# A hybrid decoder layer on one core: gate tiles moved ahead of and behind a block inverse, gate sends moved to ScalarE, HGRN's early decays moved last in order, and down weights loaded into four idle slots

## The chip, the core and the metric

The kernel runs on one core of one Trainium2 chip. The core has TensorE for matrix products, VectorE and ScalarE for elementwise work, GpSimd, and queues from which transfers are started: SyncE's, ScalarE's and GpSimd's. All operands are float32; a product of two of them is made of three matmuls on "hi" and "lo" parts (rounded value and remainder) in a reduced float32 format. The metric is device time of one execution in microseconds (us); lower is better.

## What is computed

One decoder layer on 512 tokens of width 1024. Two causal mixers run on the same normalised input, a gated linear recurrence (HGRN2) and a gated delta rule (DeltaNet), both in 4 heads of 128. Their outputs are projected, weighted with the sigmoid gates `m_a` and `m_b`, added, projected again and put on the residual; a gated feed-forward part of width 2816 follows.

```python
u = rms_norm(x, pre_mix_w)
(hg_q, hg_f, hg_i, hg_g, dn_q, dn_k, dn_v, dn_g, dn_a, dn_b, m_a, m_b) = split(u @ w_in)
o_a = head_rms_norm(hgrn2_mix(hg_q, hg_f, hg_i, lb), hg_norm_w) * silu(hg_g)
cq, ck, cv = split(silu(causal_short_conv([dn_q, dn_k, dn_v], conv_w)))
o_b = head_rms_norm(gated_deltanet_mix(cq, ck, cv, dn_a, dn_b), dn_norm_w) * silu(dn_g)
merged = sigmoid(m_a) * (o_a @ w_o_hg) + sigmoid(m_b) * (o_b @ w_o_dn)
h = x + rms_norm(merged @ w_out, post_mix_w)
gate, up = split(rms_norm(h, pre_ffn_w) @ w_gate_up)
out = h + rms_norm((silu(gate) * up) @ w_down, post_ffn_w)
```

DeltaNet needs, for each chunk of the sequence and each head, the inverse of a unit triangular matrix.

## The kernel before

**Dense tiles.** `dense_in(name, evac, fts=...)` makes tiles of 128 output columns by 512 tokens. Each takes 24 matmuls of 512 columns (8 blocks of the inner dimension, three each: lines 124 and 125), a weight block of 512 KB that `wload` brings into one of two `raw` buffers by SyncE's queue and splits into `whi` (a cast on ScalarE, line 116) and `wlo` (a subtraction on VectorE, line 117), and an evacuation `evac`. `self.log[name]` keeps the matmuls. `dn_k`, `hg_f`, `dn_q`, `dn_v`, `dn_g`, `hg_q`, `hg_g`, `m_b0`, `m_b1`, `m_a0`, `m_a1` are such groups of four tiles; `y_proj` makes `y0` (DeltaNet's output projection) and `y1` (HGRN's) of eight tiles with 12 matmuls each.

**Order.** A scheduler of the framework sets each engine's instruction order at build time from the program order, `high_priority` and `issue_after` (this instruction comes behind that one in the order; not a wait on the chip). On the chip each engine runs its own list in order and waits on semaphores. Small matmuls of the mixers stand between dense ones. The inverse (`dn_inv`) puts each of its 28 groups of products (line 493, and transposes, line 520) behind every third matmul of the list it is given. HGRN's matmuls are put behind every fifth dense matmul of the list `dense` (`FIRST`, `PACE`, `paced`).

**Around the inverse.** `dn_sub` inverts blocks of 32 on GpSimd, a long chain of small operations on one tile; the result goes to DRAM (lines 474, 476) and comes back into the two tiles that `dn_inv` multiplies (lines 497, 500), all on GpSimd's queue. `dn_prep(c)` makes the scaled operands of DeltaNet for chunk c (lines 548, 552); `dn_step(c)` is the serial recurrence (lines 568 to 588, with ScalarE copies at 573 and 578 and the state update on VectorE at line 157); `head_norm` ends it with a column sum on TensorE (lines 389, 390), and `y0` needs its output of all chunks. `hg_prep` makes HGRN's cumulative decays (lines 624 to 641), `hg_decay` one level of its decay factors (line 654). `hg_attn` and `hg_step` are HGRN's matmuls (lines 690 to 732).

**Sends.** Gate and query tiles that come before their place is free go through one spill tile `out` to DRAM (`early_q`, `early_g`, `early_b`, `early_a`) and are read back later by GpSimd's queue. `early_q` is sent by ScalarE's queue (line 795), the others by GpSimd's (lines 801, 828).

**Down projection.** `down` takes 22 weight rows of 512 KB twice, once per half of the tokens; the last four of the second pass are split into `held` tiles. Each row is loaded into one of the two `raw` buffers; a row's 12 matmuls are lines 1204 to 1206, the left operand is cast at line 1194.

The lines that set the inverse's place, the early HGRN work and the paced list are:

```python
last = self.dn_inv((self.log["hg_q"] + self.log["hg_g"])[60::3])
with self.tc.issue_after(last.ins), self.tc.issue_after(norm[1].ins):
    self.hg_prep((2, 3))
    early_e = {lev: self.hg_decay(0, lev) for lev in HG_LEVELS[:5]}
...
dense = self.log["hg_g"][48:] + self.log["y0"] + self.log["m_b1"] + self.log["m_a0"]
self.marks = iter(dense[FIRST::PACE])
```

Of the kernel before, what the change touches and what calls it, by code (L numbers as in the profile page):

```python
# [25 lines left out]
NEG = -30000.0  # L26
FIRST, PACE = 8, 5
# [20 lines left out]
class K:  # L48
# [58 lines left out]
    def wload(self, src, shape, offs=(0, 0)):  # L107

        nc = self.nc
        n = shape[1] * shape[2]  # L110
        with self.tc.high_priority():
            raw = self.wp.tile([P, 1024], F32, tag="raw", name=self.name("raw"), bufs=2)
            hi, lo = (self.wp.tile([P, WCOLS], F32R, tag=t, name=self.name(t), bufs=3)[:, o:o + 1024]
                      for t, o in zip(("whi", "wlo"), offs))
            nc.sync.dma_start(out=raw[:, :n], in_=src)
            nc.scalar.copy(hi[:, :n], raw[:, :n])  # L116
            nc.vector.tensor_tensor(out=lo[:, :n], in0=raw[:, :n], in1=hi[:, :n].bitcast(F32),  # L117
                                    op=ALU.subtract)
        r = lambda t: t[:, :n].rearrange("p (a b) -> p a b", a=shape[1])
        return r(hi), r(lo)  # L120
# [632 lines left out]
    def mixers(self):  # L753
# [23 lines left out]
        with self.tc.issue_after(norm[0].ins), self.tc.issue_after(norm[1].ins):  # L777
# [12 lines left out]
                                              for n, t in ((4, "q"), (2, "g"), (4, "b"), (4, "a")))  # L790
# [6 lines left out]
        def gge(i, ps):  # L797
            t = self.spill()
            self.sigmoid(t, ps)
            self.stt(t, ps, self.hnw, t, ALU.mult, ALU.mult)  # L800
            nc.gpsimd.dma_start(out=early_g[i], in_=t)
# [6 lines left out]
        last = self.dn_inv((self.log["hg_q"] + self.log["hg_g"])[60::3])  # L808
        with self.tc.issue_after(last.ins), self.tc.issue_after(norm[1].ins):
            self.hg_prep((2, 3))  # L810
            early_e = {lev: self.hg_decay(0, lev) for lev in HG_LEVELS[:5]}
# [10 lines left out]
        run(prev)  # L822

        def gate_out(to):
            def f(ft, ps):
                t = self.spill()
                self.sigmoid(t, ps)
                nc.gpsimd.dma_start(out=to[ft], in_=t)
            return f

        self.dense_in("m_b0", gate_out(early_b))
# [25 lines left out]
        self.dense_in("m_a0", gate_out(early_a))  # L857
        dense = self.log["hg_g"][48:] + self.log["y0"] + self.log["m_b1"] + self.log["m_a0"]
# [14 lines left out]
        nc.gpsimd.dma_start(out=self.ma[0], in_=early_a.rearrange("f p t -> p f t"))  # L873
        self.dense_in("m_a1", lambda ft, ps: self.sigmoid(self.ma[1][:, ft, :], ps))
# [36 lines left out]
    def out_proj(self):  # L911
# [47 lines left out]
        for c in range(NC_):  # L959
# [9 lines left out]
            cut = ((0, 6), (1, 6), (0, 8), (1, 8)) if c == 0 else ((0, 8), (1, 4), (2, 0), (1, 8))  # L969
# [211 lines left out]
    def down(self):  # L1181
# [25 lines left out]

        def load(k):

            with self.tc.issue_after(made[k - 2].ins) if k > 1 else nullcontext():  # L1210
                return [x[:, 0] for x in self.wload(self.I["w_down"][k], (P, 1, D))]
# [37 lines left out]
        for k in range(NF):  # L1249
            a = left(k, 1)  # L1250
            if k < NF - KT:
                w = load(k)
            else:
                i = k - NF + KT
                with now():
                    raw = self.wp.tile([P, 1024], F32, tag="raw", name=self.name("raw"), bufs=2)
                    nc.sync.dma_start(out=raw, in_=self.I["w_down"][k])
                    w = [held[j][i // 2][:, i % 2] for j in range(2)]
                    self.split(*w, raw)
                late.append((a, w))  # L1260
# [35 lines left out]
    def run(self):  # L1296
        for f in (self.consts, self.start, self.mixers, self.merge, self.out_proj, self.ffn, self.down):
            f()
# [56 lines left out]
```

## Time and profile before

| what | us |
|---|---|
| time, median of 3 runs (lowest, highest) | 843.47 (842.88, 844.0) |
| the profiled execution, its own time | 843.4 |
| its span, first to last instruction | 841.6 |
| TensorE busy in the span (96%) | 811.4 |
| VectorE busy (69%) | 581.6 |
| ScalarE busy (58%) | 490.0 |
| GpSimd busy (10%) | 86.7 |

The span starts with the loads and the normalisation, the mixers run to about 412 us, the output projection and the feed-forward part follow, and the down projection runs from 700 us to the end. A matmul's busy time as recorded overlaps that of the next, so a TensorE that looks busy may still lose time; the distance between the starts of two matmuls tells more.

### The profile page before, as it was taken

How to read it: one execution, taken by the hardware profiler on the slowest of the kernel's cores; microseconds unless marked ns; L12 is line 12 of the kernel's file. 1: busy time of each engine (PE TensorE's matmuls, PEld its weight loads, DVE VectorE, ACT ScalarE, POOL GpSimd, SP SyncE). 2: the span in 40 equal slices, each digit the busy share in tenths (PEclk: the TensorE clock that was granted, in tenths of full speed). 3: DMA queues.
4: the chain of work that ended last, by engine and by line, in shares of the span. 5: the costliest groups of instructions: out<-in, count | busy, mean ns of one | idle time of the engine just before them, and what ended most of it. 6: DMA issues, size and time to landing. Idle time of an engine off the chain costs nothing.

```text
span 841.6 us, 12290 instructions
## 1 busy us (share of the span) xinstructions
PE 811.4 (96%) x4677; PEld 682.7 (81%) x4677; DVE 581.6 (69%) x943; ACT 490.0 (58%) x917; POOL 86.7 (10%) x126
## 2 busy tenths in 40 slices
PE   9999999799998899999999999999999999999995
PEld 8878888666877678888888898999999998877764
DVE  4794998313955798964574697887887787557545
ACT  5748789436857456767644464655555457445443
POOL 1000068600002000005010300000000000000000
PEclk9999999979999899999999999999999999999998
DMA  8425442622224111257511313233423405556552
GB/s 305 173 76 199 122 130 79 156 92 69 95 93 150 51 51 51 76 182 244 176 62 50 123 45 122 85 104 114 125 76 100 151 22 171 173 176 209 176 176 100
DMA packets 36699, 103.77 MB, mean 123 GB/s; under 512 B 4448, under 2 KB 4864, under 8 KB 36512
## 3 DMA queue, kind: packets, MB, share of 16 engines
q1 hardware_dynamic: 32112, 88.65, 32.0%
q0 software_dynamic: 3952, 13.29, 5.5%
q10 hardware_dynamic: 576, 1.05, 0.4%
q8 instruction: 37, 0.61, 0.3%
q14 instruction: 22, 0.18, 0.1%
HBM read 94.57 MB, written 8.40 MB: 122 GB/s over the span
## 4 chain that ended last, share of the span: by engine, by line
PE 63%; DMA 14%; DVE 10%; ACT 5%; POOL 5%; issue 3%; DVEq 0%; SPq 0%; ACTq 0%; POOLq 0%
PE mm L124 18%; PE mm L125 9%; DMA raw<-in_w_down_dram 8%; POOL s L154 4%; DVE wlo L117 3%; PE hps L124 3%; DVE s L154 3%; ACT whi L116 2%; PE hps L1090 2%; PE hps L1089 2%; PE hps L1091 2%; DVE s L157 2%; PE hps L697 2%; PE mm L947 2%; PE mm L945 2%
## 5 line engine op out<-in xcount | busy, mean ns | idle before, releaser
L124 PE MATMUL mm<-s,whi 128*128 128x512 f32 (+1 forms) x992 | 317.5, 394 | 6.2 <-ACT s L128 5.8
L124 PEld LDWEIGHTS mm<-s,whi 128*128 128x128 f32 x992 | 184.2, 190 | 43.1 <-ACT s L128 6.6
L117 DVE TENSOR_TENSOR wlo<-raw,whi 128x1024 fp32r<-128x1024 f32 x108 | 133.2, 1233 | 124.3 <-ACT whi L116 123.0
L125 PE MATMUL mm<-s,wlo 128*128 128x512 f32 (+1 forms) x496 | 193.4, 390 | 0.0
L116 ACT CAST whi<-raw 128x1024 fp32r<-128x1024 f32 x108 | 113.3, 1049 | 78.1 <-DMA raw<-in_w_down_dram 34.8
L125 PEld LDWEIGHTS mm<-s,wlo 128*128 128x128 f32 x496 | 94.6, 191 | 16.6 <-DVE wlo L117 0.4
L128 ACT CAST whi<-s 128x512 fp32r<-128x512 f32 x42 | 26.0, 618 | 45.5 <-PE mm L124 21.0
L128 ACT CAST whi<-raw 128x512 fp32r<-128x512 f32 x56 | 34.0, 618 | 25.9 <-PE mm L1090 9.5
L1090 PE MATMUL hps<-s,whi 128*128 128x256 f32 x168 | 46.5, 277 | 0.6 <-DVE s L154 0.6
L1089 PE MATMUL hps<-s,whi 128*128 128x256 f32 x168 | 46.5, 277 | 0.4 <-DVE hct L154 0.4
L1091 PE MATMUL hps<-s,wlo 128*128 128x256 f32 x168 | 46.4, 276 | 0.0
L124 PE MATMUL hps<-s,whi 128*128 128x512 f32 (+1 forms) x144 | 40.3, 366 | 0.0
L154 DVE TENSOR_TENSOR wlo<-raw,whi 128x512 fp32r<-128x512 f32 x56 | 37.9, 687 | 1.7 <-ACT whi L128 1.0
L154 DVE TENSOR_TENSOR s<-s,s 128x512 fp32r<-128x512 f32 (+2 forms) x51 | 35.7, 711 | 2.9 <-ACT s L128 1.7
L154 POOL TENSOR_TENSOR s<-s,dct 128x256 f32<-128x256 f32 x1 | 1.2, 1208 | 353.1 <-DVE s L157 353.1
L154 POOL TENSOR_TENSOR s<-s 128x126 f32<-128x126 f32 (+22 forms) x62 | 35.1, 566 | 9.7 <-DMA s<-scr 4.9
L128 ACT CAST s<-s 128x512 fp32r<-128x512 f32 (+1 forms) x32 | 19.8, 620 | 24.6 <-DVE s L154 17.6
L1090 PEld LDWEIGHTS hps<-s,whi 128*128 128x128 f32 x168 | 31.5, 188 | 1.1 <-DVE s L154 0.8
L1089 PEld LDWEIGHTS hps<-s,whi 128*128 128x128 f32 x168 | 31.5, 188 | 0.8 <-DVE hct L154 0.6
L1091 PEld LDWEIGHTS hps<-s,wlo 128*128 128x128 f32 x168 | 31.5, 188 | 0.0
L1089 PE MATMUL mm<-s,whi 128*128 128x256 f32 x112 | 31.0, 276 | 0.0
L1091 PE MATMUL mm<-s,wlo 128*128 128x256 f32 x112 | 31.0, 276 | 0.0
(316 smaller groups left out, 1819.6 us busy)
## 6 DMA issues: line engine op xcount, KB each, us to landing
raw<-in_w_in_a_dram SPq DMA_DIRECT2D x44, 512.0 KB, 3.5
raw<-in_w_down_dram SPq DMA_DIRECT2D x44, 512.0 KB, 3.4
s<-in_w_gu_dram SPq DMA_DIRECT2D x56, 256.0 KB, 4.0
raw<-in_w_gu_dram SPq DMA_DIRECT2D x16, 512.0 KB, 3.6
raw<-in_w_o_dram SPq DMA_DIRECT2D x8, 512.0 KB, 4.2
dct<-in_w_out_dram SPq DMA_DIRECT2D x16, 256.0 KB, 5.9
s<-in_w_iab_dram SPq DMA_DIRECT2D x8, 260.0 KB, 6.6
s<-in_xT_dram SPq DMA_DIRECT2D x8, 256.0 KB, 7.3
```

Source lines behind the costliest of these rows:

```text
L116: nc.scalar.copy(hi[:, :n], raw[:, :n])
L117: nc.vector.tensor_tensor(out=lo[:, :n], in0=raw[:, :n], in1=hi[:, :n].bitcast(F32), op=ALU.subtract)
L124: return [mm(ps, lh, rh, start=start, stop=False), mm(ps, lh, rl, start=False, stop=False), mm(ps, ll, rh, start=False, stop=stop)]
L125: mm(ps, ll, rh, start=False, stop=stop)]
L128: self.nc.scalar.copy(hi, src)
L154: return (eng or self.nc.vector).tensor_tensor(out=out, in0=a, in1=b, op=op)
L157: self.nc.vector.scalar_tensor_tensor(out=out, in0=a, scalar=s, in1=b, op0=op0, op1=op1)
L697: T.matmul(ps[:, h, :], E[:, h, :], E[:, h, :], start=True, stop=True)
L945: T.matmul(ps, mh, wh, start=k == 0, stop=False)
L1089: mm(ps, wh[:, k, :], ah[k], start=start and k == 0, stop=False, skip_group_check=True)
L1090: mm(ps, wh[:, k, :], al[k], start=False, stop=False, skip_group_check=True)
L1091: mm(ps, wl[:, k, :], ah[k], start=False, stop=k == 3, skip_group_check=True)
```

## The change

Five things change. (1) Two tiles of `m_b0` stand in program order ahead of `dn_inv`, and the inverse's products begin behind the 93rd matmul of `hg_q`, `hg_g` and `m_b0` (`INV` = 92) instead of the 61st of `hg_q` and `hg_g`. (2) Behind the inverse stand the other two tiles of `m_b0` and three tiles of `m_a0`; `m_a0`'s fourth and `m_a1`'s first come behind `m_b1`, and the latter is sent to DRAM too, so `m_a1` has three tiles left. The list that paces HGRN is shortened by two tiles and ends with `m_a1`'s first. (3) `early_b` and `early_a` are sent by ScalarE's queue, `early_g` by SyncE's; GpSimd's queue sends none of them. (4) `hg_prep((2, 3))` and the five early decays stand behind DeltaNet's steps in program order. On VectorE ten of their instructions (two groups of four, lines 635 and 641 before, and two single ones) now stand between DeltaNet's first state copy and its next state update, where none stood. (5) In `down`, raw rows go into slots 5, 1, 2, 3, two rows each, in place of the two `raw` buffers. In the output projection the second column half makes 6 instead of 4 of its 8 blocks ahead of the transposes of the chunk before. The number of instructions of every engine's arithmetic stays as it was.

```diff
+INV = 92
...
-    def wload(self, src, shape, offs=(0, 0)):
+    def wload(self, src, shape, offs=(0, 0), raw=None):
...
-            raw = self.wp.tile([P, 1024], F32, tag="raw", name=self.name("raw"), bufs=2)
+            if raw is None:
+                raw = self.wp.tile([P, 1024], F32, tag="raw", name=self.name("raw"), bufs=2)
...
-                                              for n, t in ((4, "q"), (2, "g"), (4, "b"), (4, "a")))
+                                              for n, t in ((4, "q"), (2, "g"), (4, "b"), (5, "a")))
...
             self.stt(t, ps, self.hnw, t, ALU.mult, ALU.mult)
-            nc.gpsimd.dma_start(out=early_g[i], in_=t)
+            nc.sync.dma_start(out=early_g[i], in_=t)
+
+        def gate_out(to):
+            def f(ft, ps):
+                t = self.spill()
+                self.sigmoid(t, ps)
+                A.dma_start(out=to[ft], in_=t)
+            return f
...
         self.dense_in("hg_g", gge, fts=range(2))
-        last = self.dn_inv((self.log["hg_q"] + self.log["hg_g"])[60::3])
-        with self.tc.issue_after(last.ins), self.tc.issue_after(norm[1].ins):
-            self.hg_prep((2, 3))
-            early_e = {lev: self.hg_decay(0, lev) for lev in HG_LEVELS[:5]}
+        self.dense_in("m_b0", gate_out(early_b), fts=range(2))
+        last = self.dn_inv((self.log["hg_q"] + self.log["hg_g"] + self.log["m_b0"])[INV::3])
         for c in range(NC_):
             self.dn_prep(c)
...
         run(prev)
-
-        def gate_out(to):
-            def f(ft, ps):
-                t = self.spill()
-                self.sigmoid(t, ps)
-                nc.gpsimd.dma_start(out=to[ft], in_=t)
-            return f
-
-        self.dense_in("m_b0", gate_out(early_b))
+        with self.tc.issue_after(last.ins), self.tc.issue_after(norm[1].ins):
+            self.hg_prep((2, 3))
+            early_e = {lev: self.hg_decay(0, lev) for lev in HG_LEVELS[:5]}
+
+        self.dense_in("m_b0", gate_out(early_b), fts=range(2, 4))
+        self.dense_in("m_a0", gate_out(early_a), fts=range(3))
...
         self.dense_in("m_b1", gate_b)
-        self.dense_in("m_a0", gate_out(early_a))
-        dense = self.log["hg_g"][48:] + self.log["y0"] + self.log["m_b1"] + self.log["m_a0"]
+        self.dense_in("m_a0", gate_out(early_a), fts=(3,))
+        self.dense_in("m_a1", lambda ft, ps: gate_out(early_a)(4, ps), fts=(0,))
+        dense = self.log["hg_g"][48:] + self.log["y0"] + self.log["m_b1"] + self.log["m_a0"][72:] + self.log["m_a1"]
...
-        nc.gpsimd.dma_start(out=self.ma[0], in_=early_a.rearrange("f p t -> p f t"))
-        self.dense_in("m_a1", lambda ft, ps: self.sigmoid(self.ma[1][:, ft, :], ps))
+        nc.gpsimd.dma_start(out=self.ma[0], in_=early_a[:4].rearrange("f p t -> p f t"))
+        nc.gpsimd.dma_start(out=self.ma[1][:, 0], in_=early_a[4])
+        self.dense_in("m_a1", lambda ft, ps: self.sigmoid(self.ma[1][:, ft, :], ps), fts=range(1, 4))
...
-            cut = ((0, 6), (1, 6), (0, 8), (1, 8)) if c == 0 else ((0, 8), (1, 4), (2, 0), (1, 8))
+            cut = ((0, 6), (1, 6), (0, 8), (1, 8)) if c == 0 else ((0, 8), (1, 6), (2, 0), (1, 8))
...
+        rows = []
+
+        def raw(k):
+
+            if not rows or len(rows[-1]) == 2:
+                rows.append([])
+                self.rows = self.slot((5, 1, 2, 3)[(len(rows) - 1) % 4], [P, 2, D])
+            rows[-1].append(k)
+            return self.rows[:, len(rows[-1]) - 1]
+
...
-                return [x[:, 0] for x in self.wload(self.I["w_down"][k], (P, 1, D))]
+                return [x[:, 0] for x in self.wload(self.I["w_down"][k], (P, 1, D), raw=raw(k))]
...
                 with now():
-                    raw = self.wp.tile([P, 1024], F32, tag="raw", name=self.name("raw"), bufs=2)
-                    nc.sync.dma_start(out=raw, in_=self.I["w_down"][k])
+                    r_ = raw(k)
+                    nc.sync.dma_start(out=r_, in_=self.I["w_down"][k])
                     w = [held[j][i // 2][:, i % 2] for j in range(2)]
-                    self.split(*w, raw)
+                    self.split(*w, r_)
```

**TensorE, start of the inverse.** `mm_1609`, `mm_1643` and `mm_1677` are the third and fourth tile of `hg_q` and the first of `hg_g`; `dps` is written by the inverse's products, whose operands are the tiles read back from DRAM. Before:

```order
L124 MATMUL mm_1609<-s_62_563,whi_1604 128x512
L125 MATMUL mm_1609<-s_60_561,wlo_1605 128x512
L124 MATMUL mm_1609<-s_61_562,whi_1604 128x512
L493 MATMUL dps_1750<-s_246_1745,s_122_843 32x32 x4
L124 MATMUL mm_1609<-s_63_564,whi_1604 128x512
L125 MATMUL mm_1609<-s_61_562,wlo_1605 128x512
L124 MATMUL mm_1609<-s_61_562,whi_1604 128x512
L493 MATMUL dps_1750<-s_246_1745,s_122_843 32x32 x4
```

After:

```order
L127 MATMUL mm_1643<-s_61_562,wlo_1639 128x512
L126 MATMUL mm_1643<-s_61_562,whi_1638 128x512
L126 MATMUL mm_1643<-s_63_564,whi_1638 128x512
L127 MATMUL mm_1643<-s_61_562,wlo_1639 128x512
L495 MATMUL dps_1822<-s_256_1817,s_122_843 32x32 x4
L126 MATMUL mm_1643<-s_61_562,whi_1638 128x512
L126 MATMUL mm_1643<-s_63_564,whi_1638 128x512
L127 MATMUL mm_1643<-s_61_562,wlo_1639 128x512
L495 MATMUL dps_1822<-s_256_1817,s_122_843 32x32 x4
```

The first product stood behind the 13th matmul of `hg_q`'s third tile and now stands behind the 21st of its fourth, 32 dense matmuls later.

**TensorE, end of DeltaNet.** `dps` with `onesr` is the last `head_norm`'s column sum. `mm_2460` before is the last tile of `hg_g` and `mm_2498` the first of `y0`, which reads DeltaNet's normalised output (`s_300`, `s_301`). `mm_2454` and `mm_2490` after are the second and third tile of `m_a0`. Before:

```order
L389 MATMUL dps_2260<-dct_2256,onesr 128x512
L124 MATMUL mm_2460<-s_63_564,whi_2455 128x512
L125 MATMUL mm_2460<-s_61_562,wlo_2456 128x512
L124 MATMUL mm_2460<-s_61_562,whi_2455 128x512
L124 MATMUL mm_2460<-s_63_564,whi_2455 128x512
L390 MATMUL dps_2260<-dct_2257,onesr 128x512
L125 MATMUL mm_2460<-s_61_562,wlo_2456 128x512
L124 MATMUL mm_2498<-s_300_2075,whi_2493 128x512
L124 MATMUL mm_2498<-s_301_2076,whi_2493 128x512
L125 MATMUL mm_2498<-s_300_2075,wlo_2494 128x512
```

After:

```order
L391 MATMUL dps_2255<-dct_2251,onesr 128x512
L126 MATMUL mm_2454<-s_63_564,whi_2449 128x512
L127 MATMUL mm_2454<-s_61_562,wlo_2450 128x512
L392 MATMUL dps_2255<-dct_2252,onesr 128x512
L126 MATMUL mm_2490<-s_60_561,whi_2485 128x512
L126 MATMUL mm_2490<-s_62_563,whi_2485 128x512
L127 MATMUL mm_2490<-s_60_561,wlo_2486 128x512
L126 MATMUL mm_2490<-s_60_561,whi_2485 128x512
```

`y0` followed the last sum by one matmul; now a tile of `m_a0` and two tiles of `hg_g`, 72 matmuls that need nothing of DeltaNet, stand between them.

**SyncE, first loads of the down weights.** Before, a new `raw` buffer of two for each row:

```order
L115 DMA raw_988_6749<-in_w_down_dram 128x1024
L115 DMA raw_992_6770<-in_w_down_dram 128x1024
L115 DMA raw_996_6791<-in_w_down_dram 128x1024
L115 DMA raw_1000_6812<-in_w_down_dram 128x1024
L115 DMA raw_1004_6833<-in_w_down_dram 128x1024
L115 DMA raw_1008_6854<-in_w_down_dram 128x1024
```

After, names begin with the slot:

```order
L117 DMA s5_989_6752<-in_w_down_dram 128x1024 x2
L117 DMA s1_996_6793<-in_w_down_dram 128x1024 x2
L117 DMA s2_1003_6834<-in_w_down_dram 128x1024
L117 DMA s3_1010_6875<-in_w_down_dram 128x1024 x2
L117 DMA s5_1017_6916<-in_w_down_dram 128x1024
L117 DMA s2_1003_6834<-in_w_down_dram 128x1024
L117 DMA s5_1017_6916<-in_w_down_dram 128x1024
L117 DMA s1_1024_6957<-in_w_down_dram 128x1024 x2
L117 DMA s2_1031_6998<-in_w_down_dram 128x1024 x2
L117 DMA s3_1038_7039<-in_w_down_dram 128x1024 x2
```

Where two rows could be under way, eight can; the loads of one slot stand mostly in pairs.

## Rows read from the trace of the kernel before

**Rows 1.** The page, part 1: busy us, share and instructions of each engine.

```profile
PE 811.4 (96%) x4677; PEld 682.7 (81%) x4677; DVE 581.6 (69%) x943; ACT 490.0 (58%) x917; POOL 86.7 (10%) x126
```

**Rows 2.** Stretches: PE, PEld, DVE, ACT, POOL busy; granted clock, DMA share, GB/s.

```profile
168.00:178.00 10.00, 10.00 (x54) 6.49 (x53) 1.23 (x1) 2.95 (x7) 0.00 (x0) 0.50 0.34 101
...
208.00:270.00 62.00, 60.25 (x368) 51.38 (x369) 41.81 (x77) 44.37 (x87) 7.15 (x11) 1.00 0.30 97
270.00:276.00 6.00, 0.65 (x3) 0.19 (x1) 3.87 (x5) 5.10 (x9) 0.00 (x0) 0.85 0.76 277
276.00:281.00 5.00, 4.90 (x11) 3.22 (x12) 4.92 (x12) 1.09 (x3) 0.00 (x0) 0.50 0.00 0
281.00:370.00 89.00, 89.00 (x551) 72.09 (x550) 77.20 (x145) 56.28 (x122) 2.20 (x4) 1.00 0.20 63
...
700.00:833.00 133.00, 127.89 (x547) 98.50 (x546) 77.79 (x106) 67.00 (x110) 0.00 (x0) 1.00 0.53 172
```

**Rows 3.** Timeline of PE, start of the inverse: start us, us, instruction, idle before.

```profile
162.37 0.39 PE L124 MATMUL mm<-s,whi 128*128 128x512 f32 x1
167.74 0.63 PE L493 MATMUL dps<-s,s 32*32 32x32 f32 x8 [4.98 <-DMA s<-scr]
...
169.88 0.63 PE L493 MATMUL dps<-s,s 32*32 32x32 f32 x8
```

**Rows 4.** Timeline of POOL: the load that the inverse waits for is issued.

```profile
164.25 0.66 POOL L497 DMA_DIRECT2D s<-scr  x1 [6.24 <-DMA scr<-s]
```

**Rows 5.** Timeline of ACT: evacuations of the inverse's products, after 179 us.

```profile
183.49 0.27 ACT L515 ACTIVATE s<-dps 32x128 f32<-32x128 f32 x1 [0.99 <-PE dps L493]
184.75 0.27 ACT L515 ACTIVATE s<-dps 32x128 f32<-32x128 f32 x1 [0.98 <-PE dps L493]
```

**Rows 6.** Timeline of PE, end of DeltaNet and start of y0.

```profile
270.26 0.39 PE L125 MATMUL mm<-s,wlo 128*128 128x512 f32 x1
276.10 1.52 PE L124 MATMUL mm<-s,whi 128*128 128x512 f32 x2 [5.45 <-ACT s L128]
```

**Rows 7.** Timeline of PE in a dense stretch: three 512-column matmuls a period.

```profile
404.65 0.62 PE L124 MATMUL mm<-s,whi 128*128 128x512 f32 x2
...
405.33 0.62 PE L124 MATMUL mm<-s,whi 128*128 128x512 f32 x2
```

**Rows 8.** Timeline of ACT: a gate tile waits for the spill tile's send.

```profile
234.66 0.60 ACT L149 ACTIVATE out<-mm 128x512 f32<-128x512 f32 x1 [1.82 <-DMA early_b<-out]
```

**Rows 9.** Waits of PE, 208 to 270 us: us in total, times, longest.

```profile
PE dps L576 <- ACT dct L573: 1.5, 1, 1.5
```

**Rows 10.** The chain that ended last, around 730 us: start us, us, what.

```profile
728.50 3.33 DMA raw<-in_w_down_dram
731.91 1.06 ACT whi L116
732.99 1.23 DVE wlo L117
734.25 3.43 DMA raw<-in_w_down_dram
```

**Rows 11.** Waits of PE's weight loads, 700 to 834 us.

```profile
PEld mm L1205 <- DVE wlo L117: 6.0, 12, 1.1
PEld mm L1204 <- ACT whi L116: 2.9, 5, 1.2
PEld dps L1205 <- DVE wlo L117: 2.5, 5, 1.1
PEld dps L1206 <- DVE hct L154: 1.3, 1, 1.3
```

**Rows 12.** Groups of DVE, 206 to 276 us: count, busy us, mean ns.

```profile
L641 DVE TENSOR_TENSOR_SCAN s<-onesr,hct 128x128 f32<-128x128 f32 x8 | 2.7, 402 | 0.0
...
L635 DVE TENSOR_SCALAR s<-s,sm,sm 128x128 f32<-128x128 f32 x8 | 2.5, 341 | 0.0
```

**Rows 13.** DMA issues: KB each, median us from issue to landing.

```profile
early_q<-out ACTq DMA_DIRECT2D x4, 256.0 KB, 3.6
...
early_b<-out POOLq DMA_DIRECT2D x4, 256.0 KB, 3.2
```

## The prediction

> **What bounds the kernel now.** I read the page first: TensorE is busy 96% of the span and no other engine above 69% [rows 1]. So a gain can only come from time in which TensorE waits or runs slowly, and the reader should look for gaps between its starts, stage by stage. The timeline of TensorE gives its pace: three 512-column matmuls start every 0.68 us, 0.2267 us each [rows 7]. Against that pace three places stand out. At the start of DeltaNet's inverse a matmul starts at 162.37 us and the next at 167.74 us; it waited for the tile that comes back from DRAM [rows 3], whose load GpSimd issues only at 164.25 us, at the end of a long chain of its own [rows 4]. At the start of `y0` the starts are 270.26 and 276.10 us; the wait is for the last cast of DeltaNet's output [rows 6]. [...] The third place is the down projection, where the chain of waits is a ring of load, cast, subtraction, next load [rows 10], and TensorE's weight loads wait for the cast and the subtraction again and again [rows 11]. The stretch from 281 to 370 us, HGRN, is dense on TensorE, with VectorE busy 77.20 of 89 us [rows 2].
>
> **The inverse starts 32 matmuls later.** The gap costs 167.74 - 162.37 - 0.23 = 5.1 us [rows 3]. What ends it doesn't move: GpSimd's list up to this load is the same, and nothing in it waits for the matmuls that are put ahead. The first product now stands 32 x 0.2267 = 7.3 us further on, so TensorE reaches it at 162.6 + 7.3 = 169.9 us, 2.1 us after the tile was there. The whole gap should go, with two dense tiles as its cover; if the tile came 2 us later, the wait would begin again there. The slow clock goes with it if nothing else stops TensorE so long. Its price: a group of products with its three dense matmuls takes 169.88 - 167.74 = 2.14 us at 0.50 [rows 3] and 1.26 us at full clock [rows 5], so of the 10 us from 168 to 178 I get back 10 x (1 - 1.26 / 2.14) = 4.1 us. Together 9.2 us.
>
> **`y0` gets 72 matmuls ahead of it.** The gap is 276.10 - 270.26 - 0.23 = 5.6 us [rows 6]; 72 x 0.2267 = 16.3 us of gate and `hg_g` tiles now stand between the last column sum and `y0`. That is nearly three times the gap, so it goes. The 5 us at half clock behind it were dense matmuls, which go twice as fast: 2.5 us. Together 8.1 us.
>
> **DeltaNet's own stretch loses cover.** From the first preparation to the last column sum there stood 143 dense matmuls and now stand 96, so 47 x 0.2267 = 10.7 us less cover for the same serial steps. On VectorE the second state update now stands behind ten HGRN instructions, of which the two groups of four alone take 4 x 0.341 + 4 x 0.402 = 3.0 us [rows 12]. VectorE was busy 41.81 of 62 us here [rows 2]; the stretch should shrink to some 50 us and VectorE's part with it by two weight subtractions of 1.23 us [rows 10], so it will be at about 80%: not full, but with steps that wait for one another. The cost lies between nothing (the cover left is enough) and 10.7 us (every matmul of lost cover comes back as a wait). I take 2.5 us: about the length of the HGRN groups on one step, since the inserted work stands at different places of the later steps and there the dense matmuls between two products reach 20. Against it stands a wait that may go: ScalarE waited 1.82 us for the send of a gate tile [rows 8], with a DeltaNet copy behind it, and TensorE lost 1.5 us by that [rows 9]. The sends now start on ScalarE directly behind the tile's last operation, where GpSimd had to be told first. I count the 1.5 us as gained; it may be 0. What the sends cost ScalarE, which has 44.37 of 62 us of work there, I take as hidden.
>
> The median times to landing, 3.6 us from ScalarE's queue and 3.2 us from GpSimd's [rows 13], don't show a faster path. [...]
>
> **HGRN.** Between its first and last column sum stood 224 dense matmuls, now 267; 43 x 0.2267 = 9.7 us more cover, and perhaps 5 us more VectorE work (a few more weight subtractions and gate products). VectorE's share goes from 77.2 / 89 = 87% to about 82 / 99 = 83% [rows 2]. I price this at nothing: no gap there now, none expected. The bounds are 0 and the few us by which waits could start at the new seams. Behind HGRN fewer dense matmuls are left before `y1` (84 in place of 156, 19 us); GpSimd's read-back of `early_a` and its `w_out` subtractions wait there for the last gate sends, but `y1` starts late enough. If that cover were gone, the read-back of `early_a` would be late next.
>
> **Down projection.** A row needs 12 x 0.2267 = 2.72 us of TensorE. The ring of one buffer takes 734.25 - 728.50 = 5.75 us [rows 10], with two buffers 2.88 us a row, so 40 rows lose at least 40 x 0.16 = 6.2 us. From above: the weight loads wait 6.0 + 2.9 + 2.5 = 11.4 us for these rows [rows 11], partly beside running matmuls. By the stretch: 528 full matmuls' worth take 119.7 us of 133, with 1.3 us of the rest due to the left operand [rows 2, 11]. With eight rows under way the load (3.3 to 3.4 us) is off the ring, and what is left per row on ScalarE and VectorE is 1.06 and 1.23 us plus the small left operand, well under 2.72. SyncE's queue is blocked at the first reuse of slot 5 until the first rows are split, with row 5 queued behind it, but that row is needed some 13 us later. DMA was busy 0.53 of the time, 172 GB/s [rows 2], so it has room. I take 9 us, the middle. The change of 4 to 6 blocks in the output projection moves transposes by 12 matmuls or fewer where no wait stands out: 0.
>
> **Sum.** 843.4 (the profiled execution's own time, 0.1 below the median of the runs; 841.6 of it are the span) - 9.2 - 8.1 - 9.0 - 1.5 + 2.5 = 818.1 us. Measured differences of this kernel under 0.2%, 1.7 us, can't be told from none.
>
> **Rivals.**
> *The cover was needed.* VectorE and DeltaNet's chain give back most of the 10.7 us: then 818.1 - 2.5 + 10.7 = 826.3 us, between 822 and 829. For it: the steps are serial and VectorE's list there is mixed with HGRN work. Against it: TensorE waited only for about 1.5 us there with VectorE and ScalarE as full [rows 2, 9]. Chance 0.2.
> *The wait moves along instead of going.* If the tile of the inverse comes later too (its loads now meet a weight load that was not issued while TensorE stood still), gap and slow clock stay: 818.1 + 9.2 = 827.3 us. Chance 0.06.
> *ScalarE is held by its own sends: slower.* There is one spill tile, so a gate tile's first operation waits on ScalarE until the send before has landed, with all DeltaNet copies and weight casts behind it. Seven gate tiles go this way during DeltaNet and HGRN. Each leaves 24 x 0.2267 = 5.4 us, the tile's matmuls, less 1.9 us for the sigmoid's three ScalarE operations (estimated; the one in [rows 8] takes 0.60 us), so 3.5 us for its landing; where landings take 7.2 us on average each costs 3.7 us and the seven eat the 25.3 us. At 8 us they give 843.4 - 25.3 + 7 x 4.5 = 849.6 us. Medians of 3.2 and 3.6 us [rows 13] speak against it. Chance 0.03. The row with 1.82 us [rows 8] shows the mechanism. [...]
> *More goes than I count*: the down stage at its upper bound and no new wait in DeltaNet, 818.1 - 2.4 - 2.5 = 813.2 us, and small waits elsewhere below 811. Chance of less than 811: 0.04.
>
> **How the numbers follow.** The forecast, 818.1 us, with 811 to 822 around it, has 0.65; the two rivals at 826 to 827 have 0.26; a result below 811 has 0.04; slower 0.03; no change 0.02. The range 811 to 829 holds the forecast and the two rivals, with some room for their own spread: somewhat over 8 in 10. Faster by over 0.2%: 0.65 + 0.26 + 0.04 = 0.95; within 0.2%: 0.02; slower 0.03.
>
> **What would show it.** Right: TensorE starts the first product without an idle time of its own, near 170 us; the clock stays 1.00 from 165 to 285 us; `y0`'s first matmul has no wait; the ring of load, cast and subtraction is gone from the chain behind 700 us, and the down stretch is some 9 us shorter. Wrong: waits of TensorE for VectorE's state or for `dct` copies between 200 and 250 us, a granted clock of 0.50 in a new place, or ScalarE waiting for `early_b` or `early_a` for several us each.

## The result, and the profile after

The changed kernel took 814.6 to 839.9 us in four runs (median 828.4) where the kernel before took 840.2 to 844.0 (median 843.2); the ratio is 0.969, 95% interval 0.965 to 0.973. In a second measurement of the same kernel, of six executions from 813.1 to 843.1 us, the ratio was 0.974 (0.970 to 0.978), which is 819 us against 840.75 for the kernel before on that chip. The ratios are taken over the executions within 1.5% of the fastest, which leaves out those of 839.0 and 839.9 us of the first four and those of 826.8 and 843.1 us of the six. The prediction was 818.1 us, with 811 to 829 as its range: the ratio's 817 us lies in it, and so does the median of all four, but two of the four executions lie above it. The kernel before has no such spread. Where it comes from is shown below: in the profiled execution of 839.0 us TensorE stops for 2.1 us at the start of the inverse and then runs at a granted clock of 0.50 for over 54 us. The lines here are of an execution (813.1 us) without that stop.

The first part of its page, then its stretches (busy us of PE, PEld, DVE, ACT, POOL; granted clock, DMA share, GB/s), to be held against [rows 1, 2]:

```profile
PE 798.6 (98%) x4677; PEld 683.9 (84%) x4677; DVE 583.7 (72%) x943; ACT 485.4 (60%) x917; POOL 82.2 (10%) x117
```

```profile
160.00:170.00 10.00, 10.00 (x45) 8.26 (x44) 2.45 (x2) 3.07 (x4) 3.12 (x4) 1.00 0.80 216
170.00:180.00 10.00, 10.00 (x90) 6.42 (x88) 1.23 (x1) 3.48 (x9) 0.00 (x0) 1.00 0.66 225
208.00:250.00 42.00, 41.99 (x284) 36.95 (x283) 32.47 (x64) 31.56 (x65) 1.38 (x2) 1.00 0.21 74
250.00:290.00 40.00, 39.43 (x213) 31.96 (x212) 30.16 (x52) 27.88 (x56) 3.04 (x5) 1.00 0.46 151
290.00:370.00 80.00, 79.88 (x481) 66.44 (x480) 67.91 (x126) 51.30 (x109) 2.19 (x4) 1.00 0.23 72
684.00:805.00 121.00, 120.56 (x544) 99.87 (x542) 80.18 (x113) 64.16 (x108) 0.00 (x0) 1.00 0.51 183
```

The clock is 1.00 in all of them; both stretches at 0.50 [rows 2] are gone. The down projection, 133 us in [rows 2], fits into 121 us. The timeline of TensorE at the first products of the inverse shows them near 170 us, 1.25 us apart and with no idle time in front, where [rows 3] has 4.98 us:

```profile
170.78 0.43 PE L495 MATMUL dps<-s,s 32*32 32x32 f32 x8
...
172.03 0.43 PE L495 MATMUL dps<-s,s 32*32 32x32 f32 x8
```

The waits of TensorE between 208 and 290 us (line waited for: us in total, times, longest) are down to one, and `y0` is not among them; [rows 6, 9] had 5.45 and 1.5 us there:

```profile
PE hps L391 <- ACT dct L130: 0.6, 1, 0.6
```

The waits of its weight loads behind 684 us are one as well, where [rows 11] lists 12.7 us:

```profile
PEld dps L1212 <- DVE hct L156: 0.9, 1, 0.9
```

### The profile page after: what moved, and what is told of

Same layout as the page of the kernel before. It is cut to its first block, busy times and chain, and to the rows that moved or that the text cites. A ratio compares the mean times of both kernels' runs of the same rounds, so it can differ in the third digit from the quotient of the medians.

```text
span 837.2 us, 12276 instructions
## 1 busy us (share of the span) xinstructions
PE 822.4 (98%) x4677; PEld 697.2 (83%) x4677; DVE 585.9 (70%) x943; ACT 486.1 (58%) x917; POOL 81.8 (10%) x117
## 4 chain that ended last, share of the span: by engine, by line
PE 76%; DVE 10%; DMA 7%; ACT 4%; issue 2%; SPq 1%; DVEq 0%; ACTq 0%
PE mm L126 20%; PE mm L127 9%; DVE s L156 4%; PE hps L126 3%; DVE wlo L119 2%; PE hps L1096 2%; PE hps L1095 2%; PE hps L1097 2%; PE dps L495 2%; PE dps L1212 2%; PE mm L1210 2%; PE mm L1212 2%; PE mm L1211 2%; PE dps L1210 2%; PE dps L1211 2%
## 5 line engine op out<-in xcount | busy, mean ns | idle before, releaser
L126 PE MATMUL mm<-s,whi 128*128 128x512 f32 (+1 forms) x992 | 322.3, 404 | 0.3 <-ACT s L130 0.3
L127 PE MATMUL mm<-s,wlo 128*128 128x512 f32 (+1 forms) x496 | 197.6, 398 | 0.2 <-DVE wlo L119 0.2
L119 DVE TENSOR_TENSOR wlo<-raw,whi 128x1024 fp32r<-128x1024 f32 x68 | 86.6, 1275 | 78.8 <-ACT whi L118 78.1
L127 PEld LDWEIGHTS mm<-s,wlo 128*128 128x128 f32 x496 | 96.9, 195 | 19.1 <-DVE wlo L119 0.7
L118 ACT CAST whi<-raw 128x1024 fp32r<-128x1024 f32 x68 | 71.3, 1048 | 46.6 <-PE mm L126 31.6
L119 DVE TENSOR_TENSOR wlo<-s,whi 128x1024 fp32r<-128x1024 f32 x40 | 48.9, 1224 | 14.5 <-ACT whi L118 14.4
L156 DVE TENSOR_TENSOR s<-s,s 128x512 fp32r<-128x512 f32 (+3 forms) x55 | 40.7, 751 | 3.9 <-ACT s L130 2.9
L118 ACT CAST whi<-s 128x1024 fp32r<-128x1024 f32 x40 | 41.9, 1047 | 0.2 <-PE hps L1096 0.2
L1200 ACT CAST hct<-s 128x256 fp32r<-128x256 f32 x44 | 17.6, 406 | 41.4 <-PE mm L1212 26.2
L130 ACT CAST s<-s 128x512 fp32r<-128x512 f32 (+2 forms) x36 | 23.9, 667 | 27.2 <-DVE s L156 19.1
```

The costliest lines, as they stand in the source:

```text
L126: return [mm(ps, lh, rh, start=start, stop=False), mm(ps, lh, rl, start=False, stop=False), mm(ps, ll, rh, start=False, stop=stop)]
L127: mm(ps, ll, rh, start=False, stop=stop)]
L130: self.nc.scalar.copy(hi, src)
L156: return (eng or self.nc.vector).tensor_tensor(out=out, in0=a, in1=b, op=op)
```

## The experiments

Times are medians. The kernel before had medians of 840.75, 840.85, 840.84 and 839.98 us in the four sets of runs, so times of different sets, which ran on different chips, can be set side by side, but a difference of about 1 us between sets is not one that can be read.

**The changed kernel once more**, the run shown above.

> The changed kernel as it is, for a profile to read stage by stage. By the prediction's sum it takes 814 to 818 us, the first product of the inverse starts near 170 us without a wait, y0 starts without a wait, TensorE loses under 1 us to weights behind 700 us, and the stretch from DeltaNet's preparation to its last column sum shows about 2.5 us of waits. By the rival that the cover was needed, that stretch shows 8 to 11 us of waits and the down stage must have given more than 9 us. By the rival that ScalarE is held by sends (here those of the query tiles, which ScalarE's queue sent before, too), ScalarE waits 1 to 3 us for early_q just as the inverse's first copies stand behind it, and TensorE waits up to 2.3 us for such a copy.

Measured: 813.1 to 824.7 us in the four executions that the ratio keeps, ratio 0.974 (0.970 to 0.978). In the profiled one, the fastest, the inverse's start and `y0` are as the sum has them, and the down stage gives more than it has. The waits between 208 and 290 us are 0.6 us in sum, not 2.5 and not 8 to 11, and that one wait stands before a column sum into `hps`, which is HGRN's; DeltaNet's steps show none.

**Only the down rows.** The kernel before with `raw(k)` and its slots in `down`, nothing else:

```diff
+self.rows = self.slot((5, 1, 2, 3)[(len(rows) - 1) % 4], [P, 2, D])
...
-return [x[:, 0] for x in self.wload(self.I["w_down"][k], (P, 1, D))]
+return [x[:, 0] for x in self.wload(self.I["w_down"][k], (P, 1, D), raw=raw(k))]
```

> The kernel before with only the down rows in the four slots. The prediction prices this at -9.0 us (834.4 us, bounds 832 to 837). If the waits at the end of the held rows and the left operand's wait also go, 11 us (832 us). If the DMA engines and not the two buffers set the ring's pace, less than 3 us (840 us or more).

Measured: 829.6 us against 840.75, ratio 0.987 (0.985 to 0.989), so 11.1 us. (The 834.4 us expected are 843.4 - 9.0; from 840.75 us they would be 831.7.) The stretch from 700 us on, and some pieces of the chain that ended last behind 715 us, which is TensorE alone where [rows 10] shows load, cast and subtraction:

```profile
700.00:821.00 121.00, 120.56 (x546) 100.03 (x545) 80.17 (x112) 64.13 (x108) 0.00 (x0) 1.00 0.52 185
```

```profile
715.09 0.23 PE dps L1205
715.31 0.23 PE dps L1206
715.76 0.23 PE dps L1205
715.99 0.23 PE dps L1206
```

133 us became 121: the DMA engines had the room (busy 0.52 of the time), and the two buffers set the pace. The theory of a limit in the transfers is out.

**The inverse's place undone.** The changed kernel with its gate tiles where they are, and

```diff
-INV = 92
+INV = 60
```

> The changed kernel with the inverse's products behind the 61st dense matmul again, as before; the gate tiles stay where the change put them. The prediction prices the later start at 9.2 us (5.1 gap, 4.1 half clock), so this should take 9.2 us more than the changed kernel, about 826 us, with the wait for the tile from DRAM and 10 us of granted clock 0.50 back. If the rival that ScalarE's wait for early_q costs as much at the new place is right, the difference is 5 us or less.

Measured: 825.0 us (819.6 to 826.1). Against the changed kernel without its stop (815.0 us, next experiment) that is 9.9 us, against the mean of the four executions above, 818.8 us, it is 6.2. TensorE's timeline has the wait for the tile from DRAM back, and the stretches behind it the slow clock:

```profile
162.10 0.39 PE L126 MATMUL mm<-s,whi 128*128 128x512 f32 x1
167.22 0.63 PE L495 MATMUL dps<-s,s 32*32 32x32 f32 x8 [4.74 <-DMA s<-scr]
```

```profile
162.00:168.00 6.00, 1.26 (x12) 0.78 (x11) 0.00 (x0) 0.11 (x1) 3.12 (x4) 0.81 0.73 188
168.00:178.00 10.00, 10.00 (x48) 6.47 (x49) 1.23 (x1) 2.85 (x7) 0.00 (x0) 0.50 0.36 113
```

**What stops TensorE at the new place.** In the execution with the stop (839 us), ScalarE's timeline has the send of one query tile, the copy of the next into the one spill tile, and a copy of the inverse behind it; TensorE's has the stop, and the stretch behind it the clock:

```profile
167.56 0.33 ACTq L797 DMA_DIRECT2D early_q<-out  x1
...
174.23 0.59 ACT L796 COPY out<-mm 128x512 f32<-128x512 f32 x1 [2.75 <-DMA early_q<-out]
174.84 0.26 ACT L510 COPY dct<-dps 32x128 f32<-32x128 f32 x1
```

```profile
172.97 0.40 PE L126 MATMUL mm<-s,whi 128*128 128x512 f32 x1
175.43 0.50 PE L495 MATMUL dps<-s,s 32*32 32x32 f32 x8 [2.07 <-ACT dct L510]
```

```profile
176.00:230.00 54.00, 54.00 (x243) 33.88 (x244) 10.26 (x13) 16.68 (x38) 0.00 (x0) 0.50 0.11 38
```

The send of 256 KB held the copy of the next tile until 174.23 - 167.56 = 6.7 us after its issue, while the DMA engines were busy 0.90 of the time (168 to 176 us); `dct` waited behind that copy, and TensorE for `dct`. In the execution shown above the same copy started at 172.98 us with no wait. Over the six executions of the second measurement the mean granted clock falls as the time grows, from 0.999 (813.1 us) over 0.991 (820.4 us) and 0.987 (824.7 us) to 0.961 (843.1 us), so the slower ones among those that the ratio keeps seem to have a part of the slow clock too; they have no trace.

What differs ahead of the stop can be read, too. In the execution with the stop the copy of the third tile already waited for the send before it, so its own send was issued 0.8 us behind a weight load of 512 KB; in the one without the stop it was issued 0.8 us ahead of that load. With the stop, then without:

```profile
166.76 6.33 SPq L117 DMA_DIRECT2D raw<-in_w_in_a_dram  x2
166.95 0.59 ACT L796 COPY out<-mm 128x512 f32<-128x512 f32 x1 [1.47 <-DMA early_q<-out]
```

```profile
167.46 0.33 ACTq L797 DMA_DIRECT2D early_q<-out  x1
168.24 0.33 SPq L117 DMA_DIRECT2D raw<-in_w_in_a_dram  x1
```

In `inv104`, below, the third tile's send stands 0.7 us behind the load, in `prep_old` beside it, and both have the stop. No run was made to test whether this order decides.

This is the prediction's rival "ScalarE is held by its own sends", but with a send that stood on ScalarE's queue before, too; only now the inverse's copies stand right behind it. Two kernels test it. The first takes the copy of the fourth query tile off ScalarE, and its send off ScalarE's queue:

```diff
-            A.copy(t, ps)
-            A.dma_start(out=early_q[i], in_=t)
+            if i == 3:
+                nc.vector.tensor_copy(t, ps)
+                nc.gpsimd.dma_start(out=early_q[i], in_=t)
+            else:
+                A.copy(t, ps)
+                A.dma_start(out=early_q[i], in_=t)
```

> The changed kernel with the fourth query tile copied out by VectorE and sent by GpSimd, so that ScalarE does not wait there for the send of the third. Theory A: the executions of the changed kernel lie between 813 and 843 us because ScalarE's wait for early_q, with the inverse's copies behind it, stops TensorE for about 2 us in some of them and the granted clock falls to 0.50 behind that stop. Then this kernel has no wait of TensorE for those copies, all its executions lie within about 5 us, and the median is 813 to 816 us. Theory B: the spread has another cause (the clock falls at the inverse whatever ScalarE does). Then it is as wide as before and the median stays near 820 us or above.

Measured: 815.0 us, and 812.7 to 817.7 in all six executions. Theory A holds and B falls. By its ratio it can't be told from the changed kernel (0.970, 0.968 to 0.973); what it takes away is the spread of 30 us. Below, `q3_dve` is the base, since differences of a few us can be read on it.

The second leaves the copy on ScalarE and puts the products 12 dense matmuls later:

```diff
-INV = 92
+INV = 104
```

> The changed kernel with the inverse's products 12 dense matmuls (2.7 us) later still, so that the fourth query tile is copied out 9 matmuls ahead of the first product and a wait of ScalarE for the send lies beside dense work. Theory A (ScalarE's wait for early_q with the copies behind it makes the spread): all executions within about 5 us, median 813 to 816 us, or up to 2.7 us more if DeltaNet misses the cover. Theory B (another cause): the spread of 813 to 843 us stays. If DeltaNet's chain has become the bound, the wait behind its last column sums grows by 2 to 3 us and the time is 816 to 819 us.

Measured: 823.7 us, 814.3 to 845.5. The spread stays, as theory B had it, but the trace of the slowest execution has theory A's stop again (2.45 us, TensorE for `dct`): the send held the next copy for 175.89 - 168.84 = 7.1 us, until after the inverse's first product, which stands at 173.41 us:

```profile
168.84 0.33 ACTq L797 DMA_DIRECT2D early_q<-out  x1
...
175.89 0.59 ACT L796 COPY out<-mm 128x512 f32<-128x512 f32 x1 [3.58 <-DMA early_q<-out]
```

So the expectation by theory A was wrong in its size: with the copy 9 matmuls ahead of the first product in the order it had 9 x 0.227 = 2.0 us for the wait, which was 3.58 us long and not over when the product was done.

**HGRN's preparation in its old place.** The block was moved back ahead of DeltaNet's preparation, first in the changed kernel, then in `q3_dve`:

```diff
         last = self.dn_inv(...)
+        with self.tc.issue_after(last.ins), self.tc.issue_after(norm[1].ins):
+            self.hg_prep((2, 3))
+            early_e = {lev: self.hg_decay(0, lev) for lev in HG_LEVELS[:5]}
...
         run(prev)
-        with self.tc.issue_after(last.ins), self.tc.issue_after(norm[1].ins):
-            self.hg_prep((2, 3))
-            early_e = {lev: self.hg_decay(0, lev) for lev in HG_LEVELS[:5]}
```

> The changed kernel with hg_prep for chunks 2 and 3 and the five early decays back in front of DeltaNet's preparation in program order. The prediction blames about 2.5 us of DeltaNet's stretch on these groups standing on VectorE ahead of the second state update: then this kernel is 2 to 3 us faster than the changed one. If they cost nothing there, the times agree within 1 us; if they had delayed DeltaNet's own preparation in the old place, it is some us slower.

Measured: 820.6 to 844.3 us, ratio 0.982 (0.977 to 0.987), which overlaps that of the changed kernel; by itself inconclusive, for the same spread. The profiled execution (844.3 us, mean granted clock 0.963) has the stop, 2.7 us, and the granted clock of 0.50 behind it.

> The kernel q3_dve with hg_prep for chunks 2 and 3 and the early decays back in front of DeltaNet's preparation in program order. In the order of TensorE the last column sum then stands 263 dense matmuls behind the inverse's first product instead of 195, and y0 follows it after 5 dense matmuls instead of 73. Theory A (the move is what puts dense work between DeltaNet's end and y0): the wait of y0's operand is back with 3 to 5 us and some granted clock of 0.50 behind it, 818 to 823 us. Theory B (the prediction's: the groups on VectorE delay the second state update where the change put them): 812 to 813 us. If both hold, in between.

Measured: 822.0 us, 6.9 more than `q3_dve`. Theory A holds; B has the wrong sign. The waits of TensorE from 208 to 430 us begin with

```profile
PE mm L126 <- ACT s L130: 3.1, 1, 3.1
PE mm L955 <- ACT s L130: 1.7, 1, 1.7
PE dps L570 <- DVE s L156: 1.3, 1, 1.3
```

The first is `y0` waiting for DeltaNet's cast output; only 4 dense matmuls stand between DeltaNet's last column sum and `y0` in this trace. The third is a DeltaNet step that waits for VectorE, at 232.47 us. VectorE's timeline just before has an HGRN addition that waits for ScalarE (line 640 is in `hg_prep`), and the operand of the DeltaNet step behind it:

```profile
231.03 0.69 DVE L156 TENSOR_TENSOR hct<-hct,s 128x512 f32<-128x512 f32 x1 [1.42 <-ACT hct L640]
231.64 0.68 DVE L156 TENSOR_TENSOR s<-dps,sm 128x512 f32<-128x512 f32 x1
```

The HGRN groups do delay DeltaNet, but in the old place and not in the new one.

**Without the three tiles of `m_a0` behind the inverse.**

```diff
-        self.dense_in("m_a0", gate_out(early_a), fts=range(3))
...
-        self.dense_in("m_a0", gate_out(early_a), fts=(3,))
+        self.dense_in("m_a0", gate_out(early_a))
...
-... + self.log["m_a0"][72:] + self.log["m_a1"]
+... + self.log["m_a0"] + self.log["m_a1"]
```

> The kernel q3_dve without the three tiles of m_a0 behind the inverse (all four stand behind m_b1 again). In the order of TensorE DeltaNet's matmuls stand where they stood and y0 follows the last column sum after 3 dense matmuls instead of 73. The prediction prices the cover at 8.1 us (5.6 gap, 2.5 half clock): 823 us, with a wait of about 5 us for the cast of DeltaNet's output. If DeltaNet ends earlier than in the kernel before since less dense work stands between its steps, the wait is longer than 5.6 us; if HGRN's own matmuls, which start earlier here, fill it, under 3 us and 818 us.

Measured: 816.2 us, only 1.2 more than `q3_dve`, though the wait is back, with the slow clock behind it:

```profile
258.08 0.39 PE L127 MATMUL mm<-s,wlo 128*128 128x512 f32 x1
262.74 0.50 PE L126 MATMUL mm<-s,whi 128*128 128x512 f32 x1 [4.26 <-ACT s L130]
```

```profile
262.00:266.00 4.00, 3.04 (x7) 1.87 (x8) 3.98 (x10) 1.25 (x3) 0.00 (x0) 0.68 0.40 131
```

The two profiled executions are further apart than the medians, 815.8 and 812.7 us. What comes back elsewhere can be read from the distances between TensorE's starts, summed over the span where they exceed the pace (0.227 us for 512 columns, fewer columns in proportion): this trace has 3.1 us more than that of `q3_dve`. From 250 to 290 us it has 8.2 us more, in the rest of the span 5.1 us less, 2.3 of them from 410 to 420 us, where `q3_dve` waits once in the output projection. So part of what the tiles give at `y0` is missing later; which later wait each of them would have covered is not shown.

**The sends back on GpSimd** (`q3_dve` with `nc.gpsimd.dma_start` for `early_b`, `early_a` and `early_g`):

```diff
-                A.dma_start(out=to[ft], in_=t)
+                nc.gpsimd.dma_start(out=to[ft], in_=t)
...
-            nc.sync.dma_start(out=early_g[i], in_=t)
+            nc.gpsimd.dma_start(out=early_g[i], in_=t)
```

> The kernel q3_dve with the sends of early_b, early_a and early_g back on GpSimd's queue. The prediction counted 1.5 us for the sends on ScalarE: then this kernel takes 816 to 817 us and TensorE waits about 1.5 us for a copy of DeltaNet behind a late gate tile. [...] If the sends on ScalarE's queue cost it time, this kernel is faster, below 814 us.

Measured: 810.8 us (810.2 to 812.8), 4.2 less. That part of the change costs time. The wait at 236 us [rows 9] doesn't come back, so the sends were not what took it away. The two profiled executions are 2.3 us apart (812.7 and 810.4 us) and their summed distances 2.4 us, 1.3 of them between 230 and 300 us; the rest of the 4.2 us lies in executions without a trace. From 208 to 300 us ScalarE waits 1.4 us for the landing of gate tiles in `q3_dve` and 0.6 us here. The order of ScalarE's own instructions moved with the edit, so whether it is the queue or that order that costs is not settled.

**The output projection's cut** back from 6 to 4 blocks:

```diff
-... ((0, 8), (1, 6), (2, 0), (1, 8))
+... ((0, 8), (1, 4), (2, 0), (1, 8))
```

> The kernel q3_dve with 4 instead of 6 blocks of the second column half ahead of the transposes, as before. The prediction prices the change at nothing: 814 to 816 us. If the one wait of 0.8 to 1.9 us in the output projection (TensorE for ScalarE's cast near 417 us) comes from the longer cut, it is gone here and the time is 1 to 1.5 us lower; if the cut hides the transposes of chunks 1 to 3, waits of about 1 us each come back and it is 2 to 3 us higher.

Measured: 814.8 us against 815.0, no difference, as predicted; the wait near 417 us stays.

**Where that last wait comes from.** In `q3_sends_pool` the timelines of VectorE and of GpSimd show two weight subtractions that take 6.34 us together, while four subtractions of `w_out` run on GpSimd:

```profile
385.64 6.34 DVE L119 TENSOR_TENSOR wlo<-raw,whi 128x1024 fp32r<-128x1024 f32 x2 [1.56 <-ACT whi L118]
```

```profile
384.72 5.04 POOL L156 TENSOR_TENSOR s<-dct,s 128x512 fp32r<-128x512 f32 x4
```

On top of `q3_sends_pool`, all subtractions of `w_out` go to VectorE:

```diff
-                self.split(h_[:, j, :], l_[:, j, :], raw, nc.gpsimd if i % 2 else None)
+                self.split(h_[:, j, :], l_[:, j, :], raw)
```

> The kernel q3_sends_pool with all w_out subtractions on VectorE, none on GpSimd. There a weight subtraction of VectorE that takes 1.2 us elsewhere took 5.2 us while four subtractions of GpSimd of 1.3 us each ran, ahead of the one wait in the output projection (TensorE for ScalarE's cast, 1.0 us). Theory A (the two engines hold each other up, and this delay is the wait): no subtraction of VectorE over 2.5 us there, the wait near 415 us is gone, 809 to 810 us (1 to 1.5 us less than 810.8). Theory B (VectorE's own list is the bound there and takes eight more subtractions of 0.69 us): the wait is longer, 811 to 815 us. Theory C (the wait comes from the transfers of w_out): unchanged.

Measured: 809.5 us (808.9 to 810.4), 1.3 less than `q3_sends_pool`, but the kernel before was 0.9 us less in this set as well, and the ratios, 0.964 and 0.965, can't be told apart. What the trace shows is that TensorE has no wait between 380 and 430 us. VectorE's timeline at the same place:

```profile
386.64 1.23 DVE L119 TENSOR_TENSOR wlo<-raw,whi 128x1024 fp32r<-128x1024 f32 x1 [0.26 <-ACT whi L118]
387.78 0.68 DVE L156 TENSOR_TENSOR s<-dct,s 128x512 fp32r<-128x512 f32 x1
```

What theory A says of VectorE is shown, that GpSimd is held up too is not, and neither is a gain in time: an operation that GpSimd does in 1.26 us takes VectorE 0.68, and on GpSimd the four had cost VectorE 6.34 - 2 x 1.23 = 3.9 us.

**Two tiles of cover instead of three**, on top of that:

```diff
-        self.dense_in("m_a0", gate_out(early_a), fts=range(3))
+        self.dense_in("m_a0", gate_out(early_a), fts=range(2))
...
-        self.dense_in("m_a0", gate_out(early_a), fts=(3,))
+        self.dense_in("m_a0", gate_out(early_a), fts=(2, 3))
...
-... + self.log["m_a0"][72:] + self.log["m_a1"]
+... + self.log["m_a0"][48:] + self.log["m_a1"]
```

> The kernel wout_dve with two instead of three tiles of m_a0 behind the inverse, so that 48 instead of 72 dense matmuls stand between DeltaNet's last column sum and y0 (10.9 us in place of 16.3). The kernel q3_y0_old, with none, took 1.2 us more than q3_dve: 4.4 us of wait for y0's operand and slow clock behind it came, and some 4 us of small waits later went. If 10.9 us still cover DeltaNet's output and a part of those small waits goes: 1 to 2 us less than wout_dve. If the small waits stay: the same within 1 us. If the cover is too short: 2 us or more above it, with a wait for the cast of DeltaNet's output.

Measured: 808.2 us (808.0 to 808.5 in all executions), 1.3 less than `wout_dve` in the same set, and no execution of the one overlaps the other; the summed distances of the two traces differ by 1.2 us. The ratio to the kernel before is 0.962 (0.960 to 0.965). It is faster than both kernels of this case and the steadiest.

## Why the prediction was right, step by step

By the ratio the time came out where the sum put it, 0.969 x 843.2 = 817 us, but two of its terms had the wrong size, one the wrong sign and one the wrong cause, and what spreads the executions up to 843 us was not in the sum at all. One of the prediction's own signs of being wrong, a granted clock of 0.50 in a new place, showed in those executions.

- **What bounds the kernel**: right. At all three places TensorE stood or ran slowly, and there the time was gained.
- **The inverse starts later, -9.2 us**: the mechanism and the size hold (6.2 to 9.9 us by `inv60`). What the step missed is "the slow clock goes with it if nothing else stops TensorE so long": something else does, in a part of the executions. I had asked who waits for GpSimd's tile, and not what stands on ScalarE ahead of the first copies of the inverse.
- **`y0`'s cover, -8.1 us**: the gap and the slow clock are gone, and each of the two edits alone brings them back, 4.3 us of wait in `q3_y0_old` and 3.1 in `q3_prep_old`. The failed step is the cause: I put all 72 matmuls down to the tiles, but with HGRN's preparation in its old place `y0` follows DeltaNet's last sum after 4 of them, and that kernel is 6.9 us slower. And the term is a gross one: undoing the tiles costs 1.2 us net. No run undoes both edits, so the 8.1 us as a whole are not measured.
- **DeltaNet loses cover, +2.5 us**: mis-sized; between 208 and 290 us no step of DeltaNet waits, and the one wait there, 0.6 us, is HGRN's. DeltaNet's serial steps had more room than the lost 10.7 us. The reason I gave, HGRN groups in front of the second state update, is refuted by `q3_prep_old`: with the groups in their old place the kernel is 6.9 us slower.
- **Sends on ScalarE, -1.5 us**: wrong sign; back on GpSimd the kernel is 4.2 us faster. The wait of 1.5 us had gone for another reason, which no run names. No gain came from another issuer: 815.0 us with it (`q3_dve`), 810.8 us without (`q3_sends_pool`).
- **HGRN, 0, and behind it**: between 290 and 370 us the profile lists no wait of TensorE, as priced; the wait of 0.6 to 1.7 us in the output projection was not in the sum. It is VectorE's lost time beside GpSimd, 3.9 us in `q3_sends_pool` (the wait is gone in `wout_dve`), no late `early_a`.
- **Down projection, -9 us**: mis-sized, it measured 11.1. I took the middle between what two buffers allow and all waits of the weight loads; the upper end, 11.4, was the right one, since with eight rows under way nothing of the ring is left and the left operand's wait shrinks too, from 1.3 to 0.9 us. The stretch as a whole had said it: 133 - 119.7 - 1.3 = 12.0 us, with numbers that stood in the prediction and were not used.
- **Sum**: the mixers' terms came to -16.3 us and measured 815.0 - 829.6 = -14.6 with the stop taken out (`q3_dve`); the down stage gave 2.1 more than counted. The two errors nearly cancel, and inside the -14.6 a loss by the sends stands against a larger gain elsewhere, so that the sum came so close is partly luck.
- **Rivals**: "the cover was needed" did not happen. "ScalarE is held" did in a part of the executions, by a query tile's send, with 6.7 and 7.1 us of landing, close to the 7.2 us from which I let it decide; I had given it 0.03 since medians of 3.2 and 3.6 us stood against it. A median says little on the one landing that falls into the busiest microseconds (the DMA share was 0.90 from 168 to 176 us).

## What to carry to other kernels

When a wait of TensorE is moved away by putting dense work in front, list for the new place what stands ahead of the first small operations on each engine, and above all what there waits for a transfer. Price a cover net: the work that fills one gap may be missing in another stage. A transfer that must have landed by a point is to be priced by the load of the DMA engines at that point, not by its median: here the query tile's send that stopped TensorE held the next copy for 6.7 us at a DMA share of 0.90, and for 7.1 us at 0.92 to 0.93 (`inv104`), against a median to landing of 3.6 us [rows 13].

## What the runs showed of the hardware

- A stop of TensorE of 2.1 us at the first products was followed by 54 us at a granted clock of 0.50, with TensorE busy throughout (after 2.45 us in `inv104` by 62 us, 178 to 240); the 5.1 us stop of [rows 3] was followed by 10 us of it. So a shorter stop can cost far more: at 2.14 us for a product with its three dense matmuls in place of 1.25, 54 us at 0.50 are, as an estimate, 22 us lost.
- GpSimd held VectorE up: beside four GpSimd subtractions of 1.26 us, two VectorE subtractions that take 1.23 us each in `wout_dve` took 6.34 us together in `q3_sends_pool`. Why, no run here shows.
